# New durations and lags for float32 products in the model that orders a hybrid GLA / RWKV-7 layer

## The chip, the cores and the metric

One Trainium2 chip, one of its cores. The metric is the device time of one execution in microseconds (us), median over the runs. Engines are named as the profile names them: PE is TensorE (PEld its weight loads), DVE is VectorE, ACT is ScalarE, POOL is GpSimd, SP is SyncE, which issues all DMAs here.

## What is computed

One layer over 4096 tokens of width 1024, in float32: a normalised input goes through one projection into two groups of heads, 4 of gated linear attention and 8 of RWKV-7. Cut to what matters:

```python
h = _rmsnorm(x, norm_w)
u = (h @ w_in).astype(f32)
# GLA, chunks of the sequence
scores = jnp.where(causal, jnp.einsum('nbhid,nbhjd->nbhij', q_in, k_in), 0.0)
o_intra = jnp.einsum('nbhij,nbhjv->nbhiv', scores, vc)
# RWKV-7: state S is (value, key), one step a token
sa = jnp.einsum('bhvk,bhk->bhv', S, -kk_t)
S = S * w_t[:, :, None, :] + sa[..., None] * (kk_t * a_t)[:, :, None, :] + v_t[..., None] * k_t[:, :, None, :]
y = jnp.einsum('bhvk,bhk->bhv', S, r_t)
...
merged = jnp.concatenate([gla_out, rwkv_out], axis=-1).astype(x.dtype)
return x + merged @ w_out          # then a final _rmsnorm
```

## The kernel before

**Tiles and stages.** The sequence is cut into 8 blocks of 512 tokens; activations are kept transposed (channel on the partition, token along the row). The big projections split each float32 operand into two float16 parts and add three products (high x high, high x low, low x high), so a 128 x 512 result takes 24 pairs of products; each is done as a pair of column halves (128 rows of the array by 64 columns, twice). In the profile these are `bank<-x,wr` (RWKV inputs), `bank<-x,wg` and `bank<-wg,x` (GLA inputs), `bank<-x,wo` and, in the last block, `bank<-x,x` (output).

**RWKV.** A block has four units, one for a pair of heads; unit u is pair u % 4 of block u // 4, so there are 32 (0 to 31). A unit projects and mixes `rk`, then `r`, and DVE makes the operands `DD` (from r and rn) and `bk` (from kf, ta and rn); rn comes back from a broadcast through DRAM (`rn<-bcda`). Then come 16 score products, `bank<-DD,bk`: 64 rows by 128 columns of the array, two of them side by side, in chunks of 64 tokens. DVE copies them under a mask into `Nb` and `DD`. POOL (for unit 31 DVE) inverts the 32 x 32 blocks (`Tc`, `tm`), which go through DRAM into `Nb`; the products `bank<-Ta,Nb` and `bank<-Nb,Ta` make 64 x 64 inverses of them. Then the chunk chain runs, 8 chunks after each other, three links each: `ch<-sv,DD`, ACT copies `us`; `ch<-us,Nb`, ACT copies `uv`; `ch<-uv,bk`, DVE makes the next state `sv`. Each link is one pair of column halves in float32 (the function `duo`; the profile shows four MATMUL for it, since float32 takes two passes). The outputs are `y<-DD,sv` and `y<-Nb,uv`. In the GLA group `bank<-ident,ki`, `bank<-vt,gbc`, `bank<-qi,ki` and `bank<-SC,vt` follow each other through ACT and DVE.

**What sets the order.** Nothing is issued as the code runs. Generators for the streams (projections, units, chain, GLA, output, weights) are recorded as steps: `account` gives each step a modelled start, from which buffers, banks and a first order follow. Then `forward` orders all steps of all engines again, by lists of what is ready, with ranks that `backward` takes from the planned ends; 50 such orders are planned, and the one with the earliest modelled end is emitted. Every engine then runs its instructions strictly in that order, with semaphores for the dependences. So the constants of the model set what stands where, on PE, DVE, ACT, POOL and SP alike.

**PE in the model.** `Array.put` gives a product's modelled start and length. d is columns / 2400 + 0.0025 us (float32 counts four times); `form` is the piece of the array that is used, and a change of form adds 0.09. `full` says that all 16 tiles of the array are used, `f32` is 2 for float32 products and 1 for transposes, `self.f32` is the type of the product before. `lag` is the time from a product's end to the moment when another engine may use it. `duo` records the column halves as one step; the score products go through the general path, with form (2, 4).

Of the kernel before, what the change touches and what calls it, by code (L numbers as in the profile page):

```python
# [10 lines left out]
F32 = mybir.dt.float32  # L11
# [70 lines left out]
def hymba_kernel(ctx, tc, xT, wt, wg, wo, wua, gup, pk, ck, out):  # L82
# [34 lines left out]
    def parts(ap):  # L117
        if ap.tensor.name == out.tensor.name or ap.tensor.name.rsplit("_", 1)[0] in TABLES:
            return []
        if ap.space == DRAM:  # L120
            return dram(ap)
        a = ap.start_partition()
        tag = ap.tensor.name.rsplit("_", 1)[0].rstrip("0123456789_")
        if tag in FINE:
            q = FINE[tag]
            return [(ap.tensor.name, h) for h in range(a // q, (a + ap.shape[0] - 1) // q + 1)]
        hs = range(a // 64, (a + ap.shape[0] - 1) // 64 + 1)
        if ap.tensor.name in HEADS:
            o = ap.offset % P // 64
            e = range(2) if ap.ap[-1][1] > 64 else range(o, o + 1)  # L130
            return [(ap.tensor.name, h, i) for h in hs for i in e]
        if ap.tensor.name in XS:
            o = ap.offset % (4 * TB) // TB
            e = range(o, o + max(1, math.prod(ap.shape[1:]) // TB)) if ap.dtype == F16 else range(4)
            return [(ap.tensor.name, h, 2 + i) for h in hs for i in e]
        return [(ap.tensor.name, h) for h in hs]

    def place(eng, t, d):

        q = busy.setdefault(eng, [])  # L140
        while q and q[0][1] < now[0] - 100:
            q.pop(0)
        i = 0
        for i, (a, e) in enumerate(q):
            if t + d <= a:
                break
            t = max(t, e)
        else:
            i = len(q)
        q.insert(i, (t, t + d))  # L150
        return t

    class Array:
# [5 lines left out]
        def put(self, t, d, cols, tiles):  # L159
            r, c, f32 = tiles[:3]  # L160
            form = (r[1] - r[0], c[1] - c[0]) + tuple(tiles[3:])
            q = [(i, j) for i in range(r[0], r[1]) for j in range(c[0], c[1])]
            turn = form != self.form
            t = max([t, self.free] + [self.tile.get(k, 0.0) for k in (self.tile if turn else q)]) + 0.09 * turn
            w, k = int(t / 3.413), self.clock
            if w > k[0]:
                k[:] = [w, 0.0, w == k[0] + 1 and k[1] >= 3060]
            k[1] += cols
            d *= 1 if k[2] else 2
            full = len(q) == 16  # L170
            if full and f32 == 2:
                d += (0.02 if len(form) == 2 else 0.058 if cols <= 256 else 0.0) + (0.0 if self.f32 else 0.045)
            elif full and self.f32 and not f32:
                d += 0.017
            elif f32 and form == (2, 4):
                d += 0.036
            for k in q:
                self.tile[k] = t + (d if full or not f32 else 0.66 * d)
            self.form, self.f32 = form, f32 > 0
            self.free = t + (d if full or turn and f32 else d / 2 if f32 and form != (4, 1) else 0.014)  # L180
            return t, d
# [3 lines left out]
    def account(eng, out, ins, d, lag, cols=0, tiles=None):  # L185
        rdy = lambda k: (lambda r: r[0] + early(r[1], eng))(ready.get(k, (0.0, "")))
        t = max([0.0] + [rdy(k) for a in ins for k in parts(a)]
                + [used.get(k, 0.0) for k in parts(out)]
                + [rdy(k) for k in parts(out) if eng != "T"])
        if eng == "T":  # L190
            t0, d = array.put(max(t, now[0]), d, cols, tiles)
            t, now[0] = t0, array.free
        else:
            if eng == "D":
                t0 = place("H", t, 0.5)
                t = t0 + 1.15
            t = place(eng, t, d)
            if eng != "D":
                t0 = t
        for a in ins:  # L200
            for k in parts(a):
                used[k] = max(used.get(k, 0.0), t + d + (0.95 if eng == "D" else 0.1))
        for k in parts(out):
            ready[k] = (t + d + lag, eng)
        return t0

    def early(a, b):

        if a not in "VSGT" or b not in "VSGT" or not a:
            return 0.0  # L210
        if a == b:
            return {"V": -0.075, "S": -0.1, "G": -0.18, "T": 0.0}[a]
        return -0.045 if a == "T" else 0.0 if b == "T" else -0.04
# [198 lines left out]
    class Engine:  # L412
# [5 lines left out]
        def __getattr__(self, op):  # L418
            f = getattr(self.eng, op)

            def call(*a, **kw):
# [3 lines left out]
                if aps:  # L425
# [20 lines left out]
                    else:  # L446
# [9 lines left out]
                        if e is not None:  # L456
                            for k in parts(e):
                                ready[k] = (ready[parts(o)[0]][0] + 0.1, self.name)
                put(t0, self.name, d, lag, cols, tiles, tab, outs, ins, lambda: f(*a, **kw))  # L459

            return call
# [34 lines left out]
    V, S, G, T, D = (Engine(n, e) for n, e in (("V", nc.vector), ("S", nc.scalar), ("G", nc.gpsimd), ("T", nc.tensor), ("D", nc.sync)))  # L496
    lo, hi = slice(0, 64), slice(64, 128)

    def duo(o, outs, lhs, rhs, start, stop):

        r = rhs[0]
        n = math.prod(r.shape[1:]) * (4 if r.dtype == F32 else 1)
        a = r.start_partition() // 32
        tiles = [(a, a + r.shape[0] // 32), (0, 4), 2 * (r.dtype == F32)]
        d, cols, ins = n / 2400 + 0.0025, n * r.shape[0] / 128, list(lhs) + list(rhs)
        t0 = account("T", o, ins, d, 0.25, cols, tiles)

        def f():
            for x, l, y in zip(outs, lhs, rhs):
                nc.tensor.matmul(x, lhsT=l, rhs=y, start=start, stop=stop)  # L510

        put(t0, "T", d, 0.25, cols, tiles, None, [o], ins, f)

    def both(o, lhs, rhs, start, stop):
        duo(o, [o[h] for h in (lo, hi)], [lhs[:, h] for h in (lo, hi)], [rhs, rhs], start, stop)
# [101 lines left out]
    def all_max(m, o, st):  # L617

        yield after(m)
        ps = yield from need(st)  # L620
        duo(ps[:, 0:P], [ps[h, 0:P] for h in (lo, hi)], [m.broadcast_to((P, 64))] * 2, [ident] * 2, True, True)
        V.tensor_reduce(o, ps[:, 0:P], op=ALU.max, axis=AX.X)
        rel(st)
# [150 lines left out]
    def spread(rows, ps, heads):  # L774

        for g in range(4):
            o = ps[:, P * g:P * g + P]
            duo(o, [o[h] for h in (lo, hi)], [sel[:, g, h % heads:h % heads + 1].broadcast_to((P, 64)) for h in range(2)], [rows] * 2, True, True)
# [840 lines left out]
```

## Time and profile before

| | |
|---|---|
| median of 3 runs | 2273.74 us (2267.16 to 2278.33) |
| profiled execution | 2279.23 us |
| its span, first to last instruction | 2277.5 us |
| PE busy | 2163.2 us (95%), 30800 products |
| DVE, ACT, POOL busy | 1709.3 (75%), 1252.1 (55%), 864.3 us (38%) |
| mean granted clock of PE | 0.984 |

Busy times are unions of an engine's instructions. Products are pipelined and their ends are modelled, so where a product's price matters, starts are compared. Idle time of an engine that is not the bound costs nothing.

### The profile page before, as it was taken

What the parts mean: (1) busy time and instruction counts of PE and PEld (TensorE: products, weight loads), DVE (VectorE), ACT (ScalarE), POOL (GpSimd) and SP (SyncE); (2) the same over time, 40 slices, a digit from 0 to 9 for tenths busy, and PEclk for the clock granted to TensorE, in tenths of its full rate; (3) what the DMA queues carried; (4) which work ended last, traced back from release to release, by engine and by line L of the source; (5) the groups of instructions that cost most, each with busy time, mean ns of one, the idle gap of its engine ahead of it and who ended that gap; (6) DMA issues with size and microseconds to landing.
All of it is one profiled execution on the core that took longest, in us unless ns stands there. A gap on an engine that the chain in (4) does not pass through costs nothing.

```text
span 2277.5 us, 75271 instructions
## 1 busy us (share of the span) xinstructions
PE 2163.2 (95%) x30800; PEld 1374.7 (60%) x30800; DVE 1709.3 (75%) x3801; ACT 1252.1 (55%) x3229; POOL 864.3 (38%) x2212
## 2 busy tenths in 40 slices
PE   7989998999999999999999999999999999999986
PEld 3656655565666556666576566666666565765754
DVE  7988879478774887749777597767878488685866
ACT  7676775455554547455555456545465465554442
POOL 2460434425335252433623264342633435332400
PEclk9999999999999999999999999999999999999998
DMA  6786654355334643446434554345534465344432
GB/s 187 225 250 204 184 175 133 114 177 154 101 109 124 189 136 102 113 128 189 138 99 109 167 179 127 104 121 182 160 108 117 132 184 151 95 115 140 140 98 81
DMA packets 275455, 326.91 MB, mean 144 GB/s; under 512 B 131572, under 2 KB 132772, under 8 KB 275108
## 3 DMA queue, kind: packets, MB, share of 16 engines
q1 hardware_dynamic: 275108, 322.10, 48.0%
q8 instruction: 241, 3.95, 0.7%
q14 instruction: 106, 0.87, 0.1%
HBM read 276.94 MB, written 45.05 MB: 141 GB/s over the span
## 4 chain that ended last, share of the span: by engine, by line
PE 57%; DVE 23%; DMA 9%; ACT 6%; issue 4%; SPq 2%; DVEq 0%; ACTq 0%
PE bank L510 45%; PE bank L459 7%; PE ch L510 3%; DVE DD L459 3%; DVE nta L459 2%; DMA xr<-in_xT_dram 2%; DVE bk L459 2%; SPq L459 2%; DVE sv L459 1%; DMA rn<-bcda 1%; DMA Nb<-td 1%; DVE Nb L459 1%; PE y L459 1%; DMA crs<-bcdc 1%; PE y L510 1%
## 5 line engine op out<-in xcount | busy, mean ns | idle before, releaser
L510 PE MATMUL bank<-x,wr 128*64 128x512 f16 x6528 | 803.8, 383 | 15.0 <-DVE DD L459 9.0
L459 POOL TENSOR_TENSOR tm<-Tc,f 128x60 f32<-128x60 f32 (+24 forms) x961 | 348.7, 363 | 660.2 <-DMA f<-nd 576.3
L510 PEld LDWEIGHTS <-wr 128*64 128x64 f16 x6528 | 361.1, 111 | 267.9 <-issue 36.4
L459 POOL TENSOR_TENSOR Tc<-Tc,tm 128x60 f32<-128x60 f32 (+24 forms) x961 | 347.1, 361 | 75.0
L510 PE MATMUL bank<-x,wg 128*64 128x512 f16 x3072 | 371.7, 382 | 1.8 <-DMA wg<-wdr 1.7
L510 PE MATMUL bank<-x,wo 128*64 128x512 f16 x2976 | 354.6, 381 | 0.4 <-ACT x L459 0.3
L459 POOL TENSOR_TENSOR xacc<-xacc,xr 128x512 f32<-128x512 f32 x98 | 130.7, 1333 | 382.2 <-ACT xr L459 256.1
L510 PEld LDWEIGHTS <-wg 128*64 128x64 f16 x3072 | 167.4, 111 | 130.3 <-issue 6.4
L510 PEld LDWEIGHTS <-wo 128*64 128x64 f16 x2976 | 162.2, 110 | 112.5 <-issue 4.4
L459 DVE SCALAR_TENSOR_TENSOR sv<-ch,PC,psd 64x64 f32<-64x64 f32 x448 | 126.2, 282 | 136.2 <-PE ch L510 123.3
L510 PEld LDWEIGHTS <-x 128*64 128x64 f16 x6240 | 193.0, 111 | 30.8 <-issue 19.3
L510 PE MATMUL bank<-wg,x 128*64 128x128 f16 x6144 | 197.7, 221 | 10.2 <-DMA wg<-wdr 7.2
L459 ACT ACTIVATE psd<-sv,PC 128x128 f32<-128x128 f32 x256 | 102.5, 400 | 179.9 <-DVE sv L459 145.0
L459 ACT COPY uv<-ch 64x64 f32<-64x64 f32 x512 | 105.5, 206 | 107.5 <-PE ch L510 101.3
L459 ACT COPY us<-ch 64x64 f32<-64x64 f32 x512 | 105.2, 205 | 89.5 <-PE ch L510 79.2
L459 ACT ACTIVATE sa<-bank,mu_s 128x512 f32<-128x512 f32 x104 | 71.6, 688 | 66.8 <-PE bank L510 63.1
L510 PEld LDWEIGHTS ch<-sv,DD 128*64 128x64 f32 x1024 | 65.1, 136 | 54.1 <-DVE sv L459 31.1
L459 PE MATMUL bank<-DD,bk 64*128 64x128 f32 x1024 | 81.2, 293 | 15.1 <-DVE bk L459 11.6
L459 DVE COPY_PREDICATED Nb<-mc,bank 64x512 f32<-64x512 uint8 x128 | 92.5, 727 | 3.7 <-PE bank L459 1.8
L510 PEld LDWEIGHTS ch<-us,Nb 128*64 128x64 f32 x1024 | 66.5, 137 | 47.5 <-ACT us L459 23.1
L459 DVE COPY_PREDICATED DD<-mc,bank 64x512 f32<-64x512 uint8 x128 | 92.8, 729 | 2.4
L510 PEld LDWEIGHTS ch<-uv,bk 128*64 128x64 f32 x1024 | 66.8, 137 | 45.2 <-ACT uv L459 16.0
(333 smaller groups left out, 3569.9 us busy)
## 6 DMA issues: line engine op xcount, KB each, us to landing
wr<-wdr SPq DMA_DIRECT2D x256, 256.0 KB
wg<-wdr SPq DMA_DIRECT2D x184, 256.0 KB
xr<-in_xT_dram SPq DMA_DIRECT2D x176, 256.0 KB
wo<-wdr SPq DMA_DIRECT2D x128, 256.0 KB
f<-nd SPq DMA_DIRECT2D x128, 128.0 KB
x<-in_wt_dram SPq DMA_DIRECT2D x29, 512.0 KB
wdr<-wo SPq DMA_DIRECT2D x25, 512.0 KB
out_dram<-mgg SPq DMA_DIRECT2D x33, 256.0 KB
```

Source lines behind the costliest of these rows:

```text
L459: put(t0, self.name, d, lag, cols, tiles, tab, outs, ins, lambda: f(*a, **kw))
L510: nc.tensor.matmul(x, lhsT=l, rhs=y, start=start, stop=stop)
```

## The change

Three surcharges of the model are set anew, and a lag. A column-half float32 product costs 0.005 us over its columns instead of 0.02; the 0.045 us for a float32 product behind a float16 one and the 0.017 us for the way back are gone (so is a branch for full-array float32 products of one piece, of which there are none); a score product costs 0.008 instead of 0.036; the lag of `duo` in float32 is 0.3 instead of 0.25.

```diff
             full = len(q) == 16
             if full and f32 == 2:
-                d += (0.02 if len(form) == 2 else 0.058 if cols <= 256 else 0.0) + (0.0 if self.f32 else 0.045)
-            elif full and self.f32 and not f32:
-                d += 0.017
+                d += 0.005
             elif f32 and form == (2, 4):
-                d += 0.036
+                d += 0.008
...
-        t0 = account("T", o, ins, d, 0.25, cols, tiles)
+        lag = 0.3 if r.dtype == F32 else 0.25
+        t0 = account("T", o, ins, d, lag, cols, tiles)
...
-        put(t0, "T", d, 0.25, cols, tiles, None, [o], ins, f)
+        put(t0, "T", d, lag, cols, tiles, None, [o], ins, f)
```

The instructions are the same, 30800 products among them; their order, and which bank or buffer each uses, change on every engine. Two places show it.

DVE ahead of the score products of unit 14. Before, from the mix of r (`r<-bank`) to the last operand `bk`:

```order
L459 SCALAR_TENSOR_TENSOR r_0_199<-bank4_0_186,omu_s_0_119,sa_0_216 128x512
L459 TENSOR_TENSOR kf_0_198<-kf_0_198,rk_0_194 128x512
L459 TENSOR_TENSOR DD0_0_131<-r_0_199,EP_0_233 64x8x64
L459 SCALAR_TENSOR_TENSOR sv_1_255<-ch_0_264,PC_1_235,psd_0_266 64x64 x2
L459 SCALAR_TENSOR_TENSOR qi_0_243<-bank0_0_182,invs_0_120,gep_0_227 128x512
L459 TENSOR_TENSOR DD0_0_131<-r_0_199,EP_0_233 64x8x64
L459 TENSOR_TENSOR bk_0_241<-kf_0_198,E_0_196 64x8x64 x2
L459 SCALAR_TENSOR_TENSOR rn_0_195<-rk_0_194,pkt_0_95,rn_0_195 128x512
L459 SCALAR_TENSOR_TENSOR ta_0_197<-ta_0_197,rn_0_195 128x512
L459 TENSOR_TENSOR DD0_0_131<-rn_0_195,EP_0_233 64x8x64 x2
L459 SCALAR_TENSOR_TENSOR bk_0_241<-ta_0_197,E_0_196 64x8x64 x2
```

After, `bk` is made first, and ten rows later the mix of r follows with `DD` alone (two pieces, the second down to the masked copy of the scores):

```order
L457 SCALAR_TENSOR_TENSOR ta_0_197<-ta_0_197,rn_0_195 128x512
L457 TENSOR_TENSOR bk_0_241<-kf_0_198,E_0_196 64x8x64
L457 TENSOR_SCALAR nm_1_229<-gbc_0_226 128x4
L457 SCALAR_TENSOR_TENSOR bk_0_241<-ta_0_197,E_0_196 64x8x64 x2
L457 SCALAR_TENSOR_TENSOR mgg3_0_87<-mgg3_0_87,pkt_0_95,xacc_0_193 128x512
```

The second piece:

```order
L457 SCALAR_TENSOR_TENSOR r_0_199<-bank0_0_182,omu_s_0_119,sa_0_216 128x512
L457 TENSOR_TENSOR DD0_0_131<-r_0_199,EP_0_233 64x8x64 x2
L457 SCALAR_TENSOR_TENSOR sv_1_255<-ch_0_262,PC_1_235,psd_0_264 64x64 x2
L457 TENSOR_TENSOR DD0_0_131<-rn_0_195,EP_0_233 64x8x64 x2
L457 SCALAR_TENSOR_TENSOR ki_0_237<-bank4_0_186,invs_0_120,gbc_0_226 128x512
L457 SCALAR_TENSOR_TENSOR qi_0_243<-bank1_0_183,invs_0_120,gep_0_227 128x512
L457 COPY_PREDICATED Nb0_0_134<-mc_0_96,bank5_0_187 64x4x2x64
```

What moved: between the mix of r and the scores stand 7 DVE instructions (with x2 counted twice) instead of 15, and rn, ta and all of bk are done before r.

PE in the tail, where the chains of units 30 (`Nb_0_134`) and 31 (`Nb_0_135`) meet. Before, the 64 x 64 inverse of unit 31 stands inside a stretch of unit 30's links with no projection between them (`amo` is the scale of the last output):

```order
L510 MATMUL ch_264<-us_265,Nb_0_134 64x64 x2
L510 MATMUL ch_264<-uv_133,bk_241 64x64 x2
L510 MATMUL ch_264<-sv_254,DD_0_131 64x64 x2
L510 MATMUL ch_264<-us_265,Nb_0_134 64x64 x2
L459 MATMUL bank_0_187<-Ta_251,Nb_0_135 32x32
L510 MATMUL bank_0_185<-ident_102,amo_281 64x128 x2
L510 MATMUL ch_264<-uv_133,bk_241 64x64 x2
L459 MATMUL bank_0_187<-Ta_251,Nb_0_135 32x32 x15
L510 MATMUL ch_264<-sv_254,DD_0_131 64x64 x2
L459 MATMUL bank_0_187<-Nb_0_135,Ta_251 32x32 x16
L510 MATMUL ch_264<-us_265,Nb_0_134 64x64 x2
```

After, that stretch holds only the transposes of v and the scale, and ends with the scale ahead of the output's first products; unit 31's inverse stands some 10 us of PE work later, between output products:

```order
L509 MATMUL ch_262<-sv_254,DD_0_131 64x64 x2
L509 MATMUL ch_262<-us_263,Nb_0_134 64x64 x2
L509 MATMUL ch_262<-uv_133,bk_241 64x64 x2
L509 MATMUL ch_262<-sv_254,DD_0_131 64x64 x2
L457 MATMUL bank_0_187<-ident_102,v_200 128x128 x4
L509 MATMUL ch_262<-us_263,Nb_0_134 64x64 x2
L509 MATMUL ch_262<-uv_133,bk_241 64x64 x2
L509 MATMUL ch_262<-sv_254,DD_0_131 64x64 x2
L509 MATMUL bank_0_182<-ident_102,amo_281 64x128 x2
L509 MATMUL ch_262<-us_263,Nb_0_134 64x64 x2
L509 MATMUL ch_262<-uv_133,bk_241 64x64 x2
L509 LDWEIGHTS wo_138
```

What moved: unit 31's inverse is later, out of the bare stretch, and more of unit 30's chain lies ahead of it.

## The prediction

> **What bounds the kernel now.** I read the page first (its busy line), then the same engines in three stretches, then what TensorE (PE) waited for in the middle one.
>
> ```profile
> span 2277.5 us, 75271 instructions
> PE 2163.2 (95%) x30800; PEld 1374.7 (60%) x30800; DVE 1709.3 (75%) x3801; ACT 1252.1 (55%) x3229; POOL 864.3 (38%) x2212
> ```
>
> ```profile
> core 0: us, PE busy (x) PEld busy (x) DVE busy (x) ACT busy (x) POOL busy (x), PEclk, DMA share, GB/s
> 0.00:285.00 285.00, 251.03 (x3568) 160.02 (x3570) 242.34 (x655) 201.03 (x419) 105.03 (x245) 0.96 0.68 210
> 285.00:2150.00 1865.00, 1809.53 (x25851) 1149.71 (x25852) 1380.92 (x2918) 1002.99 (x2673) 755.42 (x1951) 0.99 0.47 137
> 2150.00:2277.50 127.50, 102.65 (x1388) 65.02 (x1385) 86.01 (x230) 48.10 (x137) 3.84 (x17) 0.90 0.32 91
> ```
>
> PE is the bound. In the middle it stands still for 1865.00 - 1809.53 = 55.5 us (3%), at the start for 34.0 us, in the tail for 24.9 us. No instruction is added or removed, so PE's work stays; an order can only win or lose part of these 114 us, plus what a change of PE's form or a slow clock costs. In the middle, PE waited for:
>
> ```profile
> PE bank L459 <- DVE bk L459: 10.4, 11, 2.7
> PE bank L510 <- DMA wg<-wdr: 8.9, 8, 2.4
> PE bank L459 <- DVE Ta L459: 7.4, 9, 2.8
> PE bank L510 <- DVE DD L459: 7.4, 6, 3.8
> PE bank L510 <- ACT gbc L459: 4.0, 3, 1.6
> PE ch L510 <- DVE sv L459: 2.9, 8, 0.7
> PE ch L510 <- ACT us L459: 1.1, 4, 0.5
> PE ch L510 <- ACT uv L459: 0.7, 2, 0.5
> ```
>
> The columns are total us, times, longest. The first row is the score products, waiting for VectorE (DVE) to finish their operands; the last three are the links of the chunk chain, 4.7 us together. About 34 us of this hangs on DVE or ScalarE, which the order decides; 9 us hangs on weight transfers.
>
> **Are the new numbers those of the trace?** In the timeline of PE (start, length, instructions), starts are compared, since ends are modelled:
>
> ```profile
> 1652.15 1.47 PE L510 MATMUL bank<-x,wr 128*64 128x512 f16 x12
> 1653.44 0.28 PE L510 MATMUL ch<-uv,bk 128*64 128x64 f32 x4
> 1653.56 1.25 PE L510 MATMUL bank<-x,wr 128*64 128x512 f16 x10
> 1654.64 0.28 PE L510 MATMUL ch<-sv,DD 128*64 128x64 f32 x4
> ...
> 1630.28 2.06 PE L459 MATMUL bank<-DD,bk 64*128 64x128 f32 x32
> 1632.27 0.84 PE L510 MATMUL bank<-x,wg 128*64 128x512 f16 x6
> ...
> 1848.67 1.16 PE L459 MATMUL bank<-DD,bk 64*128 64x128 f32 x16
> 1849.76 0.84 PE L510 MATMUL bank<-x,wr 128*64 128x512 f16 x6
> ```
>
> Six f16 pairs before a chain link take 1.29 us, five take 1.08, so 0.215 each: the link's float32 type adds nothing to its neighbour. The link takes 0.12 us from its start to the next f16 start; its modelled base is 256 / 2400 + 0.0025 = 0.109. The old surcharge made it 0.129, or 0.174 behind f16; the new makes it 0.114. Sixteen score products take 1.99 us, eight 1.09, so 0.112 each; the model's step (half of d) was 0.126 and becomes 0.112. The new numbers are right.
>
> The old model charged PE too much: 1288 column-half float32 products x 0.015, 749 of them directly behind f16 x 0.045, 977 changes back x 0.017, 768 score products x 0.014 = 80 us (counts from the order of before). Against 2163 us that is 3.7%: the planner thought PE slower than it is, so it put too little PE work in front of each product that needs a DVE or ACT result.
>
> One page speaks against this. The Trainium skill, "TensorE: Matmul & The Clock Gate", section "The mechanism" of Part 3, says that a weight load overlaps running matmuls only when the row group differs. Both column halves use all 128 rows, so by that rule each link would show its load, the 137 ns of this row, on top, the surcharges would have been too small, and the new plan would be further from the chip:
>
> ```profile
> L510 PEld LDWEIGHTS ch<-us,Nb 128*64 128x64 f32 x1024 | 66.5, 137 | 47.5 <-ACT us L459 23.1 <-issue 2.2 <-ACT psd L459 0.6
> ```
>
> The 0.12 us above leaves no room for it; by the rule the gains below vanish and the sum ends near +1.
>
> **What the new order moves.** "Cover" below is the PE work that the order puts between a product and what it depends on, counted at the prices just read, plus 0.1 us for a change of form (these two rows: two f16 pairs of 0.43 us end 0.10 us later):
>
> ```profile
> 1649.64 0.60 PE L510 MATMUL bank<-x,wr 128*64 128x512 f16 x4
> 1650.17 0.43 PE L459 MATMUL bank<-r,bones 128*32 128x128 f32 x8
> ```
>
> (1) Score products, units 6 to 30. Per unit I set the DVE work that stands between the mix of r and the scores (means by form) plus 0.69 us of ACT against the cover from the end of the r projection. Where DVE is longer, the shortages add up to 5.1 us before and 1.9 us after. Not all waits follow this: at unit 14 it was a transfer that DVE waited for.
>
> ```profile
> 1037.07 0.75 DVE L459 SCALAR_TENSOR_TENSOR r<-bank,omu_s,sa 128x512 f32<-128x512 f32 x1
> 1046.34 0.75 DVE L459 SCALAR_TENSOR_TENSOR rn<-rk,pkt,rn 128x512 f32<-128x512 f32 x1 [2.95 <-DMA rn<-bcda]
> ...
> 1051.94 0.48 PE L459 MATMUL bank<-DD,bk 64*128 64x128 f32 x2 [2.15 <-DVE bk L459]
> ```
>
> In the new order rn and both bk stand ahead of r there: about 4.3 us of DVE work is left behind r against 7.9 us of cover, so that wait should go. I take -3 us; between -6.7 (all of the 10.4 but unit 5's) and +3.
>
> (2) Other PE waits on DVE and ACT in the middle: Ta 7.4, DD 3.6 (without unit 5), gbc 4.0, chain 4.7, together 19.7 us. Mean cover grows from 2.1 to 2.4 us between the two products of the 64-block inverse, from 51.3 to 53.7 between scores and inverse, from 2.1 to 3.6 ahead of the GLA state products; the smallest fill between chain links grows from four f16 pairs to five. But at the shortest places it hardly grows (1.2 to 1.3 us in half of the GLA pairs), and the chain already waits little. I take a third, -6; between 0 and -19.7. The transfers (8.9) I leave: SP's order changes throughout, and nothing tells which way; +-5 goes into the range.
>
> (3) Units 4 and 5, where block 1 begins. Before, unit 5 stalls, and the stall costs twice:
>
> ```profile
> 387.80 0.48 PE L459 MATMUL bank<-DD,bk 64*128 64x128 f32 x2 [2.72 <-DVE bk L459]
> 389.21 3.57 PE L459 MATMUL bank<-DD,bk 64*128 64x128 f32 x30 [0.93 <-DVE bk L459]
> 397.08 6.17 PE L510 MATMUL bank<-x,wr 128*64 128x512 f16 x30 [3.81 <-DVE DD L459]
> 403.07 2.57 PE L510 MATMUL bank<-x,wo 128*64 128x512 f16 x22
> ...
> 397.00:401.00 4.00, 3.92 (x20) 2.16 (x21) 4.00 (x8) 3.75 (x7) 0.74 (x5) 0.50 0.47 86
> ```
>
> 2.72 + 0.93 + 3.81 us idle, then 15 pairs in 5.99 us at a granted clock of 0.50 instead of 3.23: 10.2 us in all. After, unit 5's shortage falls from 3.3 to 1.3 us, but unit 4 gets 5.1 us of cover against 13.3 us of DVE work: a shortage of 8.9 where there was none. Both are one lag of DVE. Up to unit 5's scores DVE has 1.5 us more to do than before, and PE has done 2.6 us more by then: I take -1; between -10 (unit 5's cost goes) and +12 (unit 4 pays 8.9 and 3 at half clock, unit 5 keeps its own). Units 0 to 3 change by less.
>
> (4) PE changes form 697 times instead of 678: 19 x 0.1 = +2. Bounds 0 and +2: a switch inside a wait is free.
>
> (5) Tail. Before, unit 30's links run bare while unit 31's inverse lands among them, each waiting:
>
> ```profile
> 2189.74 0.34 PE L510 MATMUL ch<-us,Nb 128*64 128x64 f32 x4 [0.41 <-ACT us L459]
> 2190.76 0.34 PE L510 MATMUL ch<-uv,bk 128*64 128x64 f32 x4 [0.69 <-ACT uv L459]
> 2191.91 0.34 PE L510 MATMUL ch<-sv,DD 128*64 128x64 f32 x4 [0.81 <-DVE sv L459]
> ```
>
> After, as many links run bare, and the inverse comes some 10 us of PE work later: its cover is 36.9 us instead of 33.1 (a gain up to 3.8), while unit 31's chain has 7 us less PE work spread among its 24 links. At about 1.05 us a bare link (the steps of these rows) 24 take 25 us, and 30 us of work still lies among them. I take 0; between -4 and +4.
>
> Sum: -3 - 6 - 1 + 2 + 0 = -8 us. The profiled execution took 2279.23 us (span 2277.5 and 1.7 around it), so 2271; the median of the three runs shown is 2273.74, 5.5 below it, so I forecast 2266 us.
>
> **Rivals.**
> A, much of the waiting goes: with PE's time right, terms 2 and 3 come out at their better halves (-12 and -7), -3 and +2 beside them: -20, 2254 us. For it: every mean cover grows. Against: DVE work between r and the scores grows with the cover in most units (7.1 to 11.8 us at unit 20, cover 8.3 to 17.0), so the planner spends what it gains.
> B, slower: unit 4's scores. Their cover of 5.1 us runs out 8.9 us early, PE stands still for longer than the 3.81 us after which the clock fell to 0.50 above, and pays some 3 us more: +12, with +2 for the form changes, 2288 us. It decides when terms 1 and 2 bring less than 3 us and unit 5 keeps its stall. For it: the order there. Against: DVE's total up to unit 5 is nearly the same, so the lag is moved rather than added.
> C, the change doesn't do what it says: the best of the planned orders is as good on the chip as the old one, since an engine that waits lets the others catch up; only the form changes stay: 2276 us. The page's rule on weight loads leads there too (near +1, 2275 us); the link's 0.12 us gives that alone 3 in 100.
>
> **How the numbers follow.** -8 us: 0.52, own range 2256 to 2274; A 0.18; B 0.15; C 0.15 (the rule's 0.03 in it). A change of 0.5% is 11.4 us, about what runs between 2267.16 and 2278.33 can tell from none. Faster by more, under 2262.4: A and a third of the likeliest, 0.35. Slower, over 2285.1: most of B and a little of the others, 0.17. Within: 0.48. The range reaches to A with the transfers' 5 us and some of its bound beyond, 2246, and to B, 2288.
>
> **What would show it.** Right: PE idle in 285 to 2150 near 45 us; waits for DVE bk under 7; no wait at unit 14's scores; DMA rows as before. Term 3 is wrong if unit 4's scores (near 345 us) wait over 5 us with a granted clock of 0.5 behind them and unit 5's wait too. Term 5 is wrong if the last 127 us differ by over 4. The forecast as a whole is wrong if PE's idle time in the middle grows, or if the start (scores of unit 6, at 490 us) comes over 10 us earlier or later.

## The result, and the profile after

| | before | after |
|---|---|---|
| median | 2274.47 us (2267.16 to 2280.00, 6 runs) | 2261.60 us (2259.63 to 2263.82, 6 runs) |
| profiled execution, its span | 2279.23, 2277.5 us | 2259.63, 2257.9 us |

The ratio is 0.9938, with a 95% interval of 0.9919 to 0.9957: 12.9 us less. The forecast was 2266, so the time lies in the range, 4.4 us under the number. The profiled execution of before was 4.8 us above its median and that of after the fastest of its six, so the two traces differ by 19.6 us; about 7 us of what they show is the choice of the runs. In the experiments below, one execution of the kernel over (2285.80 us) ran in a slower state; it counts in its median and not in its ratio.

The page of after, its span and busy line:

```profile
span 2257.9 us, 75272 instructions
PE 2154.3 (95%) x30800; PEld 1377.6 (61%) x30800; DVE 1706.8 (76%) x3801; ACT 1249.7 (55%) x3229; POOL 874.7 (39%) x2212
```

The same 30800 products keep PE busy for 8.9 us less, and it stands still for 103.6 instead of 114.3 us. Between fixed times, as the prediction had it:

```profile
core 0: us, PE busy (x) PEld busy (x) DVE busy (x) ACT busy (x) POOL busy (x), PEclk, DMA share, GB/s
285.00:2150.00 1865.00, 1821.48 (x26108) 1164.57 (x26106) 1394.87 (x2960) 1009.09 (x2691) 766.11 (x1967) 0.99 0.48 138
```

PE's idle time in 285 to 2150 is 43.5 us; 55.5 before, "near 45" forecast. A faster kernel holds other work in the same window, so the two are also cut where the same PE work is done (its work counted along each order at the prices read off the trace). The middle then runs from 371.2 to 2146.5 us before (first row) and from 368.9 to 2123.0 after (second row, of the other trace):

```profile
371.20:2146.50 1775.30, 1725.14 (x24725) 1096.85 (x24723) 1307.83 (x2742) 945.43 (x2513) 722.91 (x1857) 0.99 0.46 135
...
368.90:2123.00 1754.10, 1715.34 (x24748) 1097.20 (x24746) 1301.37 (x2737) 944.05 (x2512) 726.25 (x1846) 1.00 0.47 137
```

The start gives 2.3 us and the middle 21.2; the tail takes 3.9 back. (The first cut falls between units 4 and 5, where after's lead is smallest; term 3 below comes back to it.) Of the middle's 21.2 us, 11.4 are idle time (50.2 to 38.8), and 9.8 are time in which PE counts as busy. Weighted with the granted clock of each stretch, that busy time lost 10.9 us to a slow clock before and 8.0 after, which makes 2.9 of the 9.8. The links of the chain start some 3 to 4 us less late in sum, by delays too short to show as idle time (the experiments come back to them). The rest stays open. The main rows of PE's waits of after in 285 to 2150 (us in total, times, longest):

```profile
PE bank L509 <- DMA wg<-wdr: 8.1, 6, 3.2
PE bank L509 <- DVE DD L457: 6.4, 5, 2.8
PE ch L509 <- ACT us L457: 6.3, 3, 3.2
PE bank L457 <- DVE bk L457: 4.8, 11, 1.3
PE ch L509 <- ACT uv L457: 3.3, 4, 1.1
PE ch L509 <- DVE Sst L457: 1.2, 1, 1.2
PE bank L509 <- ACT gbc L457: 0.6, 1, 0.6
```

The waits of the score products (bk) fell from 10.4 to 4.8, Ta (7.4 before) has left the list, gbc fell from 4.0 to 0.6. The links of the chain went the other way: us 1.1 to 6.3 and uv 0.7 to 3.3. The place of unit 5's stall now reads:

```profile
386.94 0.48 PE L457 MATMUL bank<-DD,bk 64*128 64x128 f32 x2
...
392.81 0.44 PE L509 MATMUL bank<-ident,amo 128*64 128x128 f32 x4 [0.70 <-DVE amo L457]
393.89 0.66 PE L457 MATMUL bank<-ident,v 128*128 128x128 f32 x4 [0.64 <-DVE amo L457]
397.30 0.64 PE L509 MATMUL bank<-x,wo 128*64 128x512 f16 x2 [2.76 <-DVE DD L457]
...
397.00:401.00 4.00, 3.67 (x18) 1.82 (x20) 3.97 (x7) 4.00 (x7) 0.00 (x0) 0.57 0.37 77
```

The scores do not wait; DVE's lag comes out 10 us later, as 4.1 us instead of 7.5, and the clock still falls (0.57).

### The profile page after: what moved, and what is told of

It is laid out like the page before. It is cut to its first block, busy times and chain, and to the rows that moved or that the text cites. A ratio compares the mean times of both kernels' runs of the same rounds, so it can differ in the third digit from the quotient of the medians.

```text
span 2257.9 us, 75272 instructions
## 1 busy us (share of the span) xinstructions
PE 2154.3 (95%) x30800; PEld 1377.6 (61%) x30800; DVE 1706.8 (76%) x3801; ACT 1249.7 (55%) x3229; POOL 874.7 (39%) x2212
## 4 chain that ended last, share of the span: by engine, by line
PE 63%; DVE 21%; DMA 8%; ACT 3%; issue 3%; SPq 1%; POOL 0%; DVEq 0%; ACTq 0%; POOLq 0%
PE bank L509 50%; PE bank L457 8%; PE ch L509 4%; DMA xr<-in_xT_dram 3%; DVE DD L457 3%; DVE nta L457 2%; DVE bk L457 2%; PE y L457 1%; DVE x L457 1%; SPq L457 1%; DVE xr L457 1%; DVE sv L457 1%; DVE Nb L457 1%; PE y L509 1%; DVE mgr L457 1%
## 5 line engine op out<-in xcount | busy, mean ns | idle before, releaser
L509 PE MATMUL bank<-x,wr 128*64 128x512 f16 x6528 | 795.5, 381 | 10.4 <-DVE DD L457 5.4
L457 POOL TENSOR_TENSOR Tc<-Tc,tm 128x60 f32<-128x60 f32 (+24 forms) x961 | 357.3, 372 | 74.4
L509 PE MATMUL bank<-x,wo 128*64 128x512 f16 x2976 | 360.9, 383 | 3.4 <-DVE DD L457 2.8
L509 PEld LDWEIGHTS <-wg 128*64 128x64 f16 x3072 | 172.3, 111 | 130.5 <-issue 9.9
L509 PE MATMUL bank<-wg,x 128*64 128x128 f16 x6144 | 194.8, 220 | 11.4 <-DMA wg<-wdr 7.2
L509 PEld LDWEIGHTS ch<-us,Nb 128*64 128x64 f32 x1024 | 68.5, 138 | 48.5 <-ACT us L457 15.3
L457 PE MATMUL bank<-DD,bk 64*128 64x128 f32 x1024 | 77.7, 286 | 11.4 <-DVE bk L457 7.4
```

## The experiments

Two explanations were set against each other. One: PE's price in the model sets how much PE work ("cover") the planner leaves between dependent products; what the change brought comes from the price (of one part, or of all). The other: any nudge makes another plan, plans of equal quality differ on the chip, and the 0.6% is such a draw. Each kernel below is planned anew from its own numbers; the instructions are always the same. "Idle" is PE's idle time in 285 to 2150 us (1865.00 less PE's busy time of that row).

**One part alone.** Each of these is before with one part of the change, against before.

*The type surcharges alone (p_types).*

```diff
-d += (0.02 if len(form) == 2 else 0.058 if cols <= 256 else 0.0) + (0.0 if self.f32 else 0.045)
-            elif full and self.f32 and not f32:
-                d += 0.017
+d += (0.02 if len(form) == 2 else 0.058 if cols <= 256 else 0.0)
```

> One part alone: only the surcharges for a change of type (0.045 us behind float16, 0.017 back) are taken out of the model; 0.02, 0.036 and the lag of 0.25 stay. They are 50 of the 80 us that the old model charged too much. Theory T (the gain comes from the right price of PE's work, which puts more PE work in front of what waits): the gain goes with the modelled time removed, 50/80 of 13 us, about -8 us, ratio 0.996, with PE's waits on DVE and ACT in the middle clearly fewer. Theory L (luck of the draw: any new order lands somewhere within about 0.6% of the old one, whatever its constants): any ratio from 0.994 to 1.006, unrelated to the other parts.

Measured: 2255.90 us, ratio 0.9930 [0.9914, 0.9947], idle 46.9 us. This part alone, 50 of the 80 us of price, gives as much as all of the change: more than theory T had asked for, and just outside theory L's range. It is one plan, which was not nudged.

*The column-half surcharge alone (p_halves).*

```diff
-d += (0.02 if len(form) == 2 else 0.058 if cols <= 256 else 0.0) + (0.0 if self.f32 else 0.045)
+d += (0.005 if len(form) == 2 else 0.058 if cols <= 256 else 0.0) + (0.0 if self.f32 else 0.045)
```

> One part alone: only the price of a column-half float32 product goes from 0.02 to 0.005 over its columns (19 of the 80 us). Theory T: about -3 us, ratio 0.9985, hard to tell from 1. Theory L: anything from 0.994 to 1.006.

Measured: 2271.52 us, 0.9989 [0.9974, 1.0003], idle 44.0 us.

*The score products alone (p_scores).*

```diff
-                d += 0.036
+                d += 0.008
```

> One part alone: only the price of a score product goes from 0.036 to 0.008 (11 of the 80 us). Theory T: about -2 us, ratio 0.999. Theory L: anything from 0.994 to 1.006; a move of 0.4% or more either way for this small part would speak for it.

Measured: 2276.05 us, 1.0006 [0.9993, 1.0019], idle 49.2 us.

*The lag alone (p_lag).*

```diff
-        t0 = account("T", o, ins, d, 0.25, cols, tiles)
+        lag = 0.3 if r.dtype == F32 else 0.25
+        t0 = account("T", o, ins, d, lag, cols, tiles)
...
-        put(t0, "T", d, 0.25, cols, tiles, None, [o], ins, f)
+        put(t0, "T", d, lag, cols, tiles, None, [o], ins, f)
```

> One part alone: only the lag behind a column-half float32 product goes from 0.25 to 0.3 us; all prices of PE's work stay as before. Theory T: it can only touch the waits of the chunk chain, 4.7 us in the middle, so 0 to -3 us, ratio 0.999. Theory L: anything from 0.994 to 1.006; 0.4% or more either way would speak for it.

Measured: 2269.85 us, 0.9988 [0.9973, 1.0002], idle 54.0 us. Of the four parts only the type surcharges moved the time by more than 0.2%, as far as one plan of each can tell.

*All of the change but the lag (no_lag),* from after:

```diff
-        lag = 0.3 if r.dtype == F32 else 0.25
+        lag = 0.25
```

> The changed model without its lag: all three prices as changed, the lag of column-half float32 products back at 0.25. Theory T: the prices carry the change, 0.992 to 0.996 of before; the chain's waits (us and uv) may grow by up to 3 us against the changed kernel. Theory L: anything from 0.994 to 1.006.

Measured: 2264.53 us, 0.9976 [0.9961, 0.9990], idle 41.9 us. The new prices without the lag give less than half of the gain, though the lag alone gave nothing: the parts do not add up, the first sign of the draw.

**The draw by itself.** Nudges that leave the fit to the chip as good as it was.

*Before, nudged (j_before1).*

```diff
-d += (0.02 if len(form) == 2 else 0.058 if cols <= 256 else 0.0) + (0.0 if self.f32 else 0.045)
+d += (0.0202 if len(form) == 2 else 0.058 if cols <= 256 else 0.0) + (0.0 if self.f32 else 0.045)
...
-                d += 0.036
+                d += 0.0361
```

> The draw, measured: the model of before with two constants moved by 1% or less (0.02 to 0.0202, 0.036 to 0.0361), which changes the order but not how well the model fits. Theory T: as before within what a draw does, 0.998 to 1.002. Theory L: draws differ as much as the change did, 0.994 to 1.006.

Measured: 2275.34 us, 1.0016 [1.0000, 1.0032], idle 54.7 us. The time stays, its make-up does not: the links' waits for uv are now among the longest, and transfers of wg cost more than before.

```profile
PE bank L510 <- DMA wg<-wdr: 11.9, 9, 3.7
PE ch L510 <- ACT uv L459: 10.1, 8, 2.9
```

*After, nudged up (j_after1).*

```diff
-                d += 0.005
+                d += 0.0052
...
-                d += 0.008
+                d += 0.0081
```

> The draw on the other side: the changed model with 0.005 to 0.0052 and 0.008 to 0.0081. Theory T: the gain stays, 0.992 to 0.996 of before. Theory L: it can be lost, up to 1.0 or more.

Measured: 2282.18 us (2278.45 to 2287.20), 1.0049 [1.0031, 1.0067], idle 53.6 us: the whole gain is gone, with prices 0.1 and 0.2 ns from those of after. Two rows of its waits in the middle:

```profile
PE bank L509 <- DMA wg<-wdr: 14.3, 9, 2.9
PE ch L509 <- ACT us L457: 7.6, 6, 2.5
```

*After, nudged down (j_after2).*

```diff
-                d += 0.005
+                d += 0.0048
...
-                d += 0.008
+                d += 0.0079
```

> The changed kernel with its numbers nudged the other way: 0.0048 instead of 0.005 for column-half products, 0.0079 instead of 0.008 for score products. If the changed prices have a gain of their own, and the first nudge (1.0049) was an unlucky draw: ratio 0.991 to 0.997, PE idle in the middle 40 to 47 us. If the change is a draw around the time before: anywhere in 0.996 to 1.006, idle 47 to 56 us, the wait for wg 9 to 15 us.

Measured: 2253.58 us (2250.37 to 2259.49), 0.9927 [0.9903, 0.9950], idle 38.4 us. The ratio is the one expected if the new prices have a gain of their own. Three plans of the new prices give 0.9938, 1.0049 and 0.9927. A single plan therefore says little about its prices to within 0.6%.

**The price, over a wider span.**

*PE priced too low by as much as before was too high (over),* from after:

```diff
-                d += 0.005
+                d += -0.010 - (0.0 if self.f32 else 0.045)
+            elif full and self.f32 and not f32:
+                d -= 0.017
             elif f32 and form == (2, 4):
-                d += 0.008
+                d -= 0.020
```

> Overshoot: the changed model, with PE's work priced too low by what it was too high before (column-half float32 products 0.010 under their columns, 0.045 less behind float16, 0.017 less on the way back, score products 0.020 under). Theory T has two forms here. If a right price is what counts, the gain is lost again, 0.998 to 1.004. If it is only that a lower price puts more PE work ahead of what waits, the gain stays or grows, 0.990 to 0.995. Theory L: anything from 0.994 to 1.006.

Measured: 2242.03 us, 0.9871 [0.9849, 0.9893]. It is the fastest kernel of this study and beats both, after by 0.7% (the quotient of the two ratios). Its middle and its longest waits there:

```profile
285.00:2150.00 1865.00, 1836.34 (x26410) 1168.33 (x26408) 1424.50 (x3018) 1015.94 (x2713) 782.75 (x1967) 1.00 0.47 139
...
PE bank L459 <- DVE bk L459: 4.3, 7, 1.0
PE bank L511 <- DVE r L459: 3.9, 1, 3.9
PE bank L459 <- POOL xacc L459: 3.1, 4, 2.3
```

Idle 28.7 us, and the waits for wg are gone. A model as wrong as that of before, only the other way, thus planned the best order so far. The next kernel shows how much of that is the draw.

*The same, nudged (over_j).*

```diff
-                d += -0.010 - (0.0 if self.f32 else 0.045)
+                d += -0.0102 - (0.0 if self.f32 else 0.045)
...
-                d -= 0.020
+                d -= 0.0201
```

> The kernel with PE priced too low (2242 us, 0.987), with two of its numbers nudged: the column-half surcharge -0.0102 instead of -0.010 us, the score product -0.0201 instead of -0.020. The fit to the chip stays as it was, only the draw among equal plans changes. Cover theory (a low price for PE makes the planner leave more PE work between dependent products, which pays on the chip): the gain stays, ratio 0.982 to 0.993, PE idle in the middle (285 to 2150 us) 25 to 38 us, no transfer of wg among the two longest waits. Draw theory (two plans of the same prices differ by up to 1.1%, and 0.987 was a lucky one): ratio 0.992 to 1.004, idle 40 to 55 us, the wait for wg back at 8 to 14 us.

Measured: 2265.88 us, 0.9976 [0.9960, 0.9992], idle 51.0 us, wg back at 6.4 us, the longest wait again. Most of over's gain was its draw.

*Lower still (over_far),* against over; some 130 us under the chip by the counts of the prediction, a little less than the expectation says:

```diff
-                d += -0.010 - (0.0 if self.f32 else 0.045)
+                d += -0.025 - (0.0 if self.f32 else 0.06)
...
-                d -= 0.017
+                d -= 0.03
...
-                d -= 0.020
+                d -= 0.035
```

> PE priced lower still: column-half products 0.025 us below their columns, another 0.06 behind float16, float16 behind float32 0.03 below, score products 0.035 below; together some 140 us under the chip, where the kernel with the low price was 80 under. Cover theory: the gain grows or has reached its bound, ratio 0.980 to 0.990, PE idle in the middle 20 to 35 us. Draw theory: anywhere in 0.992 to 1.005, idle 40 to 55 us. A third theory (right prices are best, the low price only had a lucky draw): a plan so far from the chip loses, ratio over 1.003, with more PE waits on DVE.

Measured: 2264.42 us, 0.9973 [0.9958, 0.9988], idle 41.5 us. No further gain, as the draw theory has it, and no loss either, so the third theory falls.

*Before with its errors doubled (dear).*

```diff
-d += (0.02 if len(form) == 2 else 0.058 if cols <= 256 else 0.0) + (0.0 if self.f32 else 0.045)
+d += (0.035 if len(form) == 2 else 0.058 if cols <= 256 else 0.0) + (0.0 if self.f32 else 0.09)
...
-                d += 0.017
+                d += 0.034
...
-                d += 0.036
+                d += 0.064
```

> The old prices with their errors doubled: column-half products 0.035 instead of 0.02 over their columns, 0.09 instead of 0.045 behind float16, 0.034 instead of 0.017 on the way back, score products 0.064 instead of 0.036; PE is priced some 160 us too high instead of 80. The lag stays at 0.25. Cover theory: less PE work between dependent products than before, ratio 1.004 to 1.012, PE idle in the middle 60 to 75 us, the waits for bk over 10 us. Draw theory: ratio 0.995 to 1.005, idle 45 to 58 us.

Measured: 2323.07 us, 1.0236 [1.0207, 1.0265], twice what the cover theory expected and far outside any draw seen. Its middle, and its waits there:

```profile
285.00:2150.00 1865.00, 1792.02 (x25531) 1133.48 (x25527) 1355.75 (x2863) 987.35 (x2647) 733.25 (x1900) 0.99 0.45 135
...
PE bank L459 <- DVE Ta L459: 8.7, 9, 2.2
PE ch L510 <- DVE sv L459: 7.6, 19, 1.1
PE bank L459 <- DVE bk L459: 7.1, 10, 2.0
PE ch L510 <- ACT us L459: 6.7, 11, 1.7
PE bank L510 <- DMA wg<-wdr: 6.4, 8, 1.6
PE ch L510 <- ACT uv L459: 4.9, 9, 1.4
```

Idle 73.0 us. The three links wait 19.2 us against 4.7 before; the scores, where the theory expected over 10 us, wait 7.1. So the loss is there, and the place named for it was wrong. PE is also busy for 13 us more over the whole span (2176.3 against 2163.2). Counted by starts, most of that, 9 to 13 us by the choice of the usual step, are delays of the links as well, too short to show as idle time.

All together, by PE's price against the chip (the 80 us of the prediction and its parts). Cover is the mean PE work from a unit's scores to its 32 x 32 inverse products, and the fill is the PE work between chain links of the middle that all but a tenth of the gaps exceed, both from the orders (the covers in whole us come from a second count, which differs from the first by up to 0.7). A late link is one of the middle's 670 or so links that starts over 0.1 us later than links usually do behind the same kind of product (lower quartile over all fourteen traces; stretches of slow clock left out). The last column is the time of those links that start over 1 us late.

| kernel | price, us | ratio | idle, us | cover, us | fill, us | late links | over 1 us late, us |
|---|---|---|---|---|---|---|---|
| dear | +161 | 1.0236 | 73.0 | 50.1 | 0.86 | 86 | 11.4 |
| before | +80 | 1 | 55.5 | 51.3 | 0.86 | 35 | 0 |
| j_before1 | +80 | 1.0016 | 54.7 | 52.1 | 0.86 | 41 | 10.0 |
| p_lag | +80 | 0.9988 | 54.0 | 53 | 1.07 | 39 | 6.6 |
| p_scores | +70 | 1.0006 | 49.2 | 52 | 0.86 | 36 | 1.5 |
| p_halves | +61 | 0.9989 | 44.0 | 53 | 0.86 | 33 | 3.2 |
| p_types | +30 | 0.9930 | 46.9 | 53.0 | 1.07 | 21 | 2.7 |
| after | 0 | 0.9938 | 43.5 | 53.7 | 1.07 | 19 | 9.6 |
| no_lag | 0 | 0.9976 | 41.9 | 54 | 1.07 | 17 | 3.0 |
| j_after1 | 0 | 1.0049 | 53.6 | 53.1 | 1.07 | 26 | 11.8 |
| j_after2 | 0 | 0.9927 | 38.4 | 52.7 | 1.07 | 18 | 3.7 |
| over | -80 | 0.9871 | 28.7 | 57.7 | 1.07 | 14 | 0 |
| over_j | -80 | 0.9976 | 51.0 | 55.5 | 1.07 | 17 | 4.6 |
| over_far | -130 | 0.9973 | 41.5 | 58.2 | 1.07 | 15 | 1.5 |

The orders follow the price only in the large: cover is least in dear and clearly greater from -80 on, but the groups at +61 to +80 and at 0 overlap, and the lag alone gives the greater fill too (p_lag). What follows the price most plainly is on the chip: 86 late links in dear, 33 to 41 at +61 to +80, 21 at +30, 17 to 26 at 0, and 14 to 17 below. That is the part of the cover theory that holds from group to group. It is worth little time: the links that are up to 1 us late lose 14.0 us in before and 6.9 in after. The few links that are later still follow no price, and they can take that gain back.

The time falls between the groups once. The five plans at +61 to +80 lie between 0.9988 and 1.0016; of the eight at +30 and lower seven lie below all of them (mean 0.9955). That speaks for a gain of some 0.4% from a price that is not far too high, which no single plan shows. The groups were formed after the results were known, and the lag is not the same in all of them. At 0 and below the time does not follow the price: the four plans at 0 have a mean of 0.9973, the three below it 0.9940, and each of these groups scatters over 1%. At +161 the loss is plain.

Where a plan wins is not stable either. Start times at equal PE work, against before's profiled execution, which is itself 4.8 us above its median (us):

| PE work done | before at | after | j_after1 | over | dear |
|---|---|---|---|---|---|
| 300 | 371.2 | -2.3 | +4.5 | -3.3 | +15.5 |
| 600 | 710.1 | -11.6 | -4.7 | -22.9 | +12.1 |
| 1000 | 1147.3 | -25.9 | -17.4 | -40.5 | +16.0 |
| 1400 | 1568.8 | -28.1 | -8.7 | -46.2 | +28.3 |
| 2000 | 2213.9 | -24.0 | -4.4 | -46.2 | +40.5 |

j_after1 has two thirds of after's lead by 1000 us of work and then gives it back; over's lead is made by 1400; dear loses at the start and again steadily from 1000 on.

## Why the prediction was right or wrong

The time came within 4.4 us, and 2261.6 lies 0.8 us beyond the bound of "faster by over 0.5%" (2262.4), so the less likely of the two near cases came true. That it came so near was partly luck: the four plans at the new prices have ratios of 0.9927, 0.9938, 0.9976 and 1.0049, a spread of 28 us. The mechanism behind the number is only partly borne out. That a lower price leaves fewer products late holds for the chain's links from group to group of the fourteen plans; that the gain of this one plan comes from it is not shown, since a nudge of 0.2 ns takes it all away. The prediction had no term for the draw. Rival C came nearest to it ("the best of the planned orders is as good on the chip as the old one"), with 0.12 for a case that one of the four plans at price 0, j_after1, went beyond.

*The new numbers are right.* The steps of the links hold in after's trace too: 0.12 us from a link's start to the next f16 product, behind f16 on both sides.

```profile
345.88 0.28 PE L509 MATMUL ch<-uv,bk 128*64 128x64 f32 x4
346.00 0.38 PE L509 MATMUL bank<-x,wr 128*64 128x512 f16 x2
```

So the rule of the Trainium skill ("TensorE: Matmul & The Clock Gate", Part 3, "The mechanism"), that a weight load overlaps only when the row group differs, does not describe these column halves, as the prediction had it; the same section also has loads into a background weight buffer pulled ahead, and no run here tells whether these are such. The time alone would not have told: +1 us lies inside the draw.

*Term 1, scores of units 6 to 30 (-3).* By starts, what they wait beyond a product's step fell from 7.3 to 5.6 us: -1.7. The places half agree: unit 14's wait of 2.46 us became 0.40, nearly none, as predicted,

```profile
1023.31 0.48 PE L457 MATMUL bank<-DD,bk 64*128 64x128 f32 x2 [0.38 <-DVE DD L457]
```

but units 15 and 19, without a wait before, now have 0.97 each. With unit 5 the sum went from 11.2 to 5.8.

*Term 2, other waits on DVE and ACT (-6).* From 19.7 to some 15 us, so the size was near. The make-up was wrong: Ta and gbc lost 10.8 us where the covers "at the shortest places" had promised little, and the chain, which "already waits little", rose from 4.7 to 11.1 us of idle time. By starts, with the short delays in, it rose only from 14.0 to 16.5 us: there are fewer late links (19 instead of 35), but a few very late ones. Over half of the rise in idle time is one link that waits for `us` 3.23 us, and the reason is not PE's cover: ACT stood still from 486.6 us to 490.93 at an `xr` that waited for its transfer, and the copy of `us` stands behind it. (From 1555.8 us a link of the same kind waits 2.40 us, with ACT at `vt` and two `xr` first.)

```profile
490.93 0.63 ACT L457 ACTIVATE xr<-xr 128x512 f32<-128x512 f32 x1 [4.35 <-DMA xr<-in_xT_dram]
491.47 0.39 ACT L457 ACTIVATE psd<-sv,PC 128x128 f32<-128x128 f32 x1
491.76 0.41 ACT L457 COPY us<-ch 64x64 f32<-64x64 f32 x2
...
492.22 0.34 PE L509 MATMUL ch<-us,Nb 128*64 128x64 f32 x4 [3.23 <-ACT us L457]
```

Cover on PE says nothing of that: it is a transfer's delay, handed on through ACT's strict order. The prediction kept transfers as a row of their own (8.9 us, now 8.1 for wg) and so counted only those for which PE itself waits. So idle time of an engine that is not the bound is free only while nothing behind it in its order is waited for. Such stalls differ from plan to plan: j_after1 waits 14.3 us for wg in the middle and 10.0 for us and uv, over not at all for wg and 1.4 for us and uv. They do not decide the time alone: p_types waits 13.4 us for wg there and is as fast as after.

*Term 3, units 4 and 5 (-1).* The sum held, and so did the count behind it, but not at the place where the prediction looked. Unit 4's scores run without a wait, at the same time as before (346.65):

```profile
346.31 2.06 PE L457 MATMUL bank<-DD,bk 64*128 64x128 f32 x32
```

The shortage of 8.9 us counted at unit 4, which carried rival B (2288, 0.15), was paid ahead of them. From the end of the last `bank<-x,wr` before the mix of r (near 332.1 us) PE needed some 14 us to reach them, for work that the prediction counted at 5.1 us and that comes to 6.5 at the steps of the trace. It waited 3.75 us at four places, and the granted clock fell to half behind them (it was 1.00 in the same window before):

```profile
333.98 0.34 PE L509 MATMUL ch<-us,Nb 128*64 128x64 f32 x4 [0.68 <-ACT us L457]
334.86 1.37 PE L457 MATMUL y<-Nb,uv 64*64 64x64 f32 x32 [0.55 <-ACT uv L457]
337.66 0.34 PE L509 MATMUL ch<-sv,DD 128*64 128x64 f32 x4 [1.16 <-DVE Sst L457]
339.35 0.65 PE L457 MATMUL bank<-crs,bones 128*32 128x128 f32 x8 [1.36 <-ACT crs L457]
...
342.00:346.00 4.00, 4.00 (x58) 2.68 (x56) 3.89 (x7) 1.86 (x6) 0.00 (x0) 0.52 0.45 157
```

DVE was busy for 15.3 of the 16 us from 330 to 346 and finished the last operand of these scores at 346.17, 12.6 us after it began the mix of r at 333.61; 13.3 had been counted. By then PE had lost 8 to 9 us in other places, about what the scores would have waited. Unit 5's stall, for its part, shrank by 3.4 us. At equal PE work, after is 5 to 8 us ahead where before stands at 281 to 325 us, 2 to 3 at 347 to 371, and 7 to 9 at 421 to 483. So the two units together gave 1 or 2 us, and "the lag is moved rather than added", the prediction's word against rival B, is what happened. Its sign, a wait of unit 4's scores, could not show that.

*Term 4, form changes (+2).* PE's busy time fell by 8.9 us, so the 19 more changes are not to be seen by themselves.

*Term 5, tail (0, bounds -4 to +4).* It lost 3.9 us, close to the upper bound: 1.3 us more idle time and 2.6 us more in which PE counts as busy. The tail's window and two rows of PE's waits in it, first before, then after:

```profile
2146.50:2277.50 131.00, 104.98 (x1431) 66.97 (x1425) 89.33 (x236) 48.50 (x138) 6.88 (x23) 0.91 0.31 89
PE ch L510 <- DVE sv L459: 1.9, 4, 0.8
PE ch L510 <- ACT uv L459: 0.9, 2, 0.7
...
2123.00:2257.90 134.90, 107.60 (x1414) 67.27 (x1408) 92.45 (x241) 48.41 (x140) 11.52 (x32) 0.90 0.32 89
PE ch L509 <- DVE sv L457: 2.8, 3, 1.2
PE ch L509 <- ACT uv L457: 2.6, 5, 0.5
```

The links' waits for sv and uv, 2.8 us before, are 5.4, which fits unit 31's thinner chain; its better covered inverse gave 1.5 back (Ta, 1.8 to 0.3). Where the busy time comes from is open.

*Rival A (2254).* Not what this plan did. Its nudge j_after2 took that time (2253.58), which says nothing of the rival's mechanism.

## What to carry to other kernels

Where a planner's constants are changed, plan each setting several times with nudges too small to matter, and compare the groups: here one setting spread over 1.2%, twice the gain that was to be explained. A price that is much too high for the engine that bounds the kernel is the dangerous error (+161 us cost 2.4%); from slightly too high (+30) to far too low (-130) made no difference beyond the draw. Between these, at +61 to +80, the plans are some 0.4% slower on average than those at +30 and lower. And if only the fastest kernel is wanted, take the best of the measured plans, over at 2242 us, as what it is: a good draw, not a better model.

## What was not expected of the hardware

Whether the clock falls after a wait of PE is not told by its length alone. Before, the granted clock stayed at 1.00 after 2.42 us idle (first three rows). In after's trace, after 2.40 us idle with another wait of 1.92 us just ahead of it, it stood at 0.50 from 1557.6 to 1564.4 us:

```profile
1039.61 3.26 PE L510 MATMUL bank<-wg,x 128*64 128x128 f16 x110 [2.42 <-DMA wg<-wdr]
1037.50:1040.90 3.40, 1.29 (x47) 1.28 (x48) 3.32 (x7) 1.03 (x4) 0.00 (x0) 1.00 0.85 198
1040.90:1044.30 3.40, 3.40 (x101) 3.02 (x96) 2.46 (x3) 1.53 (x5) 2.99 (x2) 1.00 0.95 335
...
1554.56 0.69 PE L509 MATMUL bank<-wg,x 128*64 128x128 f16 x18 [1.92 <-issue]
1558.19 0.48 PE L509 MATMUL ch<-us,Nb 128*64 128x64 f32 x4 [2.40 <-ACT us L457]
1554.20:1557.60 3.40, 1.23 (x24) 0.96 (x23) 3.32 (x6) 1.64 (x4) 0.18 (x1) 1.00 0.49 173
1557.60:1561.00 3.40, 2.54 (x18) 1.40 (x20) 0.39 (x2) 1.32 (x5) 2.35 (x2) 0.50 0.29 92
```

The windows here are 3.4 us long because in each of the fourteen traces the granted clock changes only on a grid of 3.41 us. Of the grid's windows at full clock in which PE was busy for less than 40% of the time, 119 of 152 were followed by 0.50; of those in which it was busy for over 80%, none of 8347. So it is the idle share of a window that goes with a fall, and two short waits in one window can do what the prediction charged only to a stall of 3.8 us. The share is not all of it: the two cases shown were busy for 38% and 36% of their windows and ended differently. No run was made to test this.
